# Rotary embedding for several heads at once: first and second halves of the heads in separate projection blocks, DMAs put each head together

## The chip, the cores and the metric

One core of a Trainium2 chip runs the kernel. The metric is device time in microseconds (us) of one execution. Engines are named as in the profile: PE (TensorE, the matrix engine; PEld is its weight load), DVE (VectorE), ACT (ScalarE), POOL (GpSimd) and SP (SyncE, which issues all DMAs here).

## What is computed

One inference step of a two-layer decoder trunk in float32, for a prompt of 512 tokens and 8 sample sequences of 4 tokens: 544 tokens with the same weights. Each layer normalises x, multiplies it by `w_in` (1024 to 3584 columns), rotates queries and keys, runs four retention heads of width 128 and eight attention heads of width 64, multiplies by `w_out`, and then runs a convolutional feed-forward part (`w_up`, `w_down`). The rotation is the part that is changed:

```python
def rotary(x, pos):
    half = x.shape[-1] // 2
    inv = ROPE_THETA ** (-jnp.arange(half, dtype=jnp.float32) / half)
    ang = pos.astype(jnp.float32)[:, None] * inv[None, :]
    cos = jnp.cos(ang)[None, :, None, :]
    sin = jnp.sin(ang)[None, :, None, :]
    x1, x2 = xf[..., :half], xf[..., half:]
    return jnp.concatenate([x1 * cos - x2 * sin, x2 * cos + x1 * sin], axis=-1)
def project(h, w_in_l, pos):
    z = h @ w_in_l
    qr, kr, vr, gr, qa, ka, va = jnp.split(z, SPLITS, axis=-1)
    qr, kr = rotary(hr(qr), pos), rotary(hr(kr), pos)      # 4 heads of 128
    qa, ka = rotary(ha(qa), pos), rotary(ha(ka), pos)      # 8 heads of 64
    return qr, kr, hr(vr), gr, qa, ka, ha(va)
```

## The kernel before

Activations lie transposed: 128 features are the partitions, the 544 tokens run along the free axis, in two halves of 272. A **block** is one output of 128 columns of a weight matrix. For a `w_in` block PE runs 48 matmuls of 128x272: eight pieces of the contraction, three passes (high and low parts of weight and activation: `xh` with `wh`, `xl` with `wh`, `xh` with `wl`), two token halves. The result lies in a PSUM tile `ps`. A weight block comes in two halves of 24 matmuls each: `load_w` (line 305) loads a half six halves ahead, `split_w` (311) splits it three halves ahead, the high part on ACT (`wh`), the low part on DVE (`wl`).

The blocks of a layer's mixer run in the order that `mixer` writes out (1032 to 1041): `va`, `va`, then for each pair of attention heads `ka`, `qa` (and the later `va`), then `vr`, `kr`, `qr` of each retention head, then four gates, 28 blocks in all, and after them 16 half-sized blocks of `w_out`. A block of queries or keys holds one retention head or two attention heads. When it is done, `rotary_out` (486) takes it out of PSUM: one DVE product of full height with the cosine table (`ra`); DVE products with the sine table that read one half of a head and write to the partitions of the other half (`rb`: four of 32 partitions in an attention block, two of 64 in a retention block); and POOL adds the two, a part of 512 tokens and a part of 32. The result is the finished head tile. The tables have the norm's factor folded in, by POOL (`fold_tables`, 539).

Between the steps of this main stream other pieces of work are placed: attention of a pair of heads (`att_pair`, 544, which first copies queries and keys into high and low parts, `qq` and `kk` on ACT, `qq` and `kl` on DVE, and then runs four `att_unit` pieces: products, softmax over DVE and ACT, transposes of `p`, products with `vt`), the sample attention, the retention heads (`ret_head`, 740). Their PE work goes to PSUM tiles called `sec`. Where they stand is decided while the program is built: `Stream` (152) keeps an estimated time for each engine (`Clock`, 60, with costs in `charge`, 115) and places a piece where that estimate says that its operands are there. On the chip each engine then runs its own list in order. Attention of pairs 0 and 2 is one sequence (`pairs`, 919), of pairs 1 and 3 another, and the sample attention follows both. Tiles of one size share 51 buffers (`blk`, 245).

Of the kernel before, what the change touches and what calls it, by code (L numbers as in the profile page):

```python
# [9 lines left out]
F32 = mybir.dt.float32  # L10
# [3 lines left out]
PSUM = bass.MemoryType.PSUM  # L14
# [3 lines left out]
NT = SEQ + NB * T  # L18
HC = NT // 2
PC = SEQ // 2  # L20
SC = NB * T // 2
KB = D // 128
ZB = 28
FB = 22
GROUPS = ((0, 5), (5, 10), (10, 14), (14, 18), (18, 22))
# [34 lines left out]
class Clock:  # L60
    """Estimates when each engine reaches and ends the instructions that were traced, so that
    independent work is traced where its operands are likely to be there."""

# [30 lines left out]
class Engine:  # L94
    """Hands instructions on to an engine of the core and to the clock."""

# [55 lines left out]
class Stream:  # L152
    """Places pieces of independent work between the steps of the main product stream. A generator
    yields what its next piece needs: its kind (the tensor engine, another engine, or a condition),
    its operands and its banks of PSUM."""

# [68 lines left out]
def trunk(ctx: ExitStack, tc: tile.TileContext, xin, w_in, w_out, w_up, w_down, kc, vc, s0, sctx_d, params_d,  # L225
# [19 lines left out]
    def blk(shape, dt=F32, s="b"):  # L245
        return work.tile(shape, dt, name=name(s), tag="blk", bufs=NBLK)
# [10 lines left out]
    def store(dst, src):  # L257
        def gen():
            sp.dma_start(dst, src)
            return  # L260
            yield
        st.spawn(gen(), "store", EW("sp", src))
# [28 lines left out]

# [1 line left out]
    main = []  # L293
# [41 lines left out]

# [1 line left out]
    x = [cpool.tile([128, 2, HC], F32, name=f"x{n}") for n in range(KB)]  # L337
# [13 lines left out]

# [1 line left out]
    class Norm:  # L353
# [47 lines left out]
        def rsqrt(self, ps, shape):  # L401
            """Yields its steps; returns 1 / sqrt(mean + eps), with a Newton step on the table's value."""
            r, v, t = (blk(shape, F32, s) for s in ("rstd", "var", "tmp"))
            yield EW("act", *ps)
            for c, p in enumerate(ps):
                act.activation(r[:, c], p[:, :HC], AF.Ln, bias=eps, scale=1.0 / D)
            act.activation(r, r, AF.Exp, scale=-0.5)
            for c, p in enumerate(ps):
                dve.tensor_scalar(v[:, c], p[:, :HC], -0.5 / D, -0.5 * EPS, op0=OP.mult, op1=OP.add)
            done(len(ps))  # L410
            yield EW("dve", r)
            dve.tensor_mul(t, r, r)
            yield EW("dve", t)
            dve.tensor_mul(t, t, v)
            yield EW("dve", t)
            dve.scalar_tensor_tensor(r, t, 1.5, r, op0=OP.add, op1=OP.mult)
            return r
# [10 lines left out]
    class Last(Norm):  # L428
        """Takes the last product stream by halves of the tokens."""

# [46 lines left out]

# [1 line left out]
    def two(ap, w):  # L479
        return ap.rearrange("p (c n) -> p c n", c=2)  # L480
# [4 lines left out]

    def rotary_out(ps, cos, sin, half, dst):
        a = blk([128, 2, HC], F32, "ra")
        b = blk([128, 2, HC], F32, "rb")
        dve.tensor_mul(a, ps[:, :, :HC], cos)
        for q in range(0, 128, 2 * half):  # L490
            lo, hi = slice(q, q + half), slice(q + half, q + 2 * half)
            dve.tensor_mul(b[lo], ps[hi, :, :HC], sin[hi])
            dve.tensor_mul(b[hi], ps[lo, :, :HC], sin[lo])
        pool.tensor_add(two(dst[:, 0:SEQ], PC), a[:, :, 0:PC], b[:, :, 0:PC])
        pool.tensor_add(two(dst[:, SEQ:NT], SC), a[:, :, PC:HC], b[:, :, PC:HC])

# [27 lines left out]

# [1 line left out]
    class Layer:  # L526
# [15 lines left out]

    # prompt attention of one pair of heads
    def att_pair(L, l, hp):
# [12 lines left out]
        done(2)  # L557
        # float32 products as f32r parts: [q hi; q lo] x [k hi; k hi], then q hi x k lo
        qs, ks = [], []
# [71 lines left out]

    # sample attention of four sequences; rows are (sequence, head, token)
    def att_sample(L, l, g):
# [104 lines left out]

    # retention of one head
    def ret_head(L, l, h):  # L740
# [31 lines left out]
        done()  # L772
        # sample parts of this head
        yield PE(k, v, q, banks=1)
# [122 lines left out]

# [1 line left out]
    def mixer(l):  # L899
# [63 lines left out]
        def va(hp):  # L963
            def evac(ps):
                if hp == 0:
                    fold_tables(L, 2, norm)
                L.va[hp] = blk([128, NT], F32, "va")
                scaled_out(ps, norm.rstd, L.va[hp])
                store(kv_o[l, 1, hp], L.va[hp])
            return evac  # L970

        def ka(hp):
            def evac(ps):
                L.ka[hp] = blk([128, NT], F32, "ka")
                rotary_out(ps, *L.tab[2], 32, L.ka[hp])
                pool.tensor_copy(L.ks[:, hp, :], L.ka[hp][:, SEQ:])
                store(kv_o[l, 0, hp], L.ka[hp])
            return evac

        def qa(hp):  # L980
            def evac(ps):
                L.qa[hp] = blk([128, NT], F32, "qa")
                rotary_out(ps, *L.tab[2], 32, L.qa[hp])
                for s in range(2):
                    r = slice(64 * s, 64 * s + 64)
                    c = (2 * hp + s) * T
                    pool.tensor_copy(L.qpad[r, hp, :, c:c + T],
                                     L.qa[hp][r, SEQ:].rearrange("p (b t) -> p b t", b=NB))
                L.cat[4 + hp] = blk([128, 2, HC], F32, "cat")
                L.have.add(("qa", hp))  # L990
                if hp == 2:
                    start_ret()
                if hp == 3:
                    L.tab.pop(2)
                    rope_tables(L, l, 0)()
                    fold_tables(L, 0, norm)
            return evac

# [11 lines left out]
        def vr(h):  # L1010
            def evac(ps):
                L.vr[h] = blk([128, NT], F32, "vr")
                scaled_out(ps, norm.rstd, L.vr[h])
            return evac

        def kr(h):
            def evac(ps):
                L.kr[h] = blk([128, NT], F32, "kr")
                rotary_out(ps, *L.tab[0], 64, L.kr[h])
            return evac  # L1020

        def qr(h):
            def evac(ps):
                L.qr[h] = blk([128, NT], F32, "qr")
                rotary_out(ps, *L.tab[0], 64, L.qr[h])
                L.cat[h] = blk([128, 2, HC], F32, "catr")
                L.have.add(("qr", h))
                if h == 3:
                    L.tab.pop(0)
            return evac  # L1030

        rhs = rhs_of(norm)
        order = [(24, va(0)), (25, va(1))]
        for hp in range(4):
            order += [(24 + hp, va(hp))] * (hp > 1) + [(20 + hp, ka(hp)), (16 + hp, qa(hp))]
        for h in range(4):
            order += [(8 + h, vr(h)), (4 + h, kr(h)), (h, qr(h))]
        for h in range(4):
# [39 lines left out]

# [1 line left out]
    def ffn(l):  # L1080
# [98 lines left out]

# [1 line left out]
    first = norms[0][0]  # L1181
# [3 lines left out]
    sp.dma_start(par, params_d[:, :NPAR])  # L1185
    # keeps the tensor engine's clock up until the first operands are there
    warm = sec([128, 512])
# [32 lines left out]

    # the first two blocks run side by side while x arrives
    main[0]["pre"]()
# [40 lines left out]

    # the last products run by halves of the tokens, so that the first half's norm and output overlap the second
    main[-KB]["pre"]()
# [20 lines left out]
def _tables():  # L1286
# [51 lines left out]
    for first, half in ((0, 64), (2, 32)):  # L1338
        e = (-np.arange(half, dtype=f) / f(half)).astype(f)
        inv = np.power(10000.0, e.astype(np.float64)).astype(f)  # L1340
        ang = (p[None, :] * inv[:, None]).astype(f).astype(np.float64)
        cos, sin = _chunk(np.cos(ang).astype(f)), _chunk(np.sin(ang).astype(f))
        rope[:, first] = np.concatenate([cos] * (128 // half))
        rope[:, first + 1] = np.concatenate([sin, -sin] * (64 // half))
    return out, rope
# [8 lines left out]
def _layout(i):  # L1354
    g = {k: np.asarray(v) for k, v in i.items()}
    a = {}
    tok = np.concatenate([g["x_prompt"].reshape(SEQ, D), g["x_sample"].reshape(NB * T, D)])
    a["xin"] = _chunk(tok.T.reshape(KB, 128, NT).transpose(1, 0, 2))

    def w(n):  # L1360
# [51 lines left out]
```

## Time and profile before

| what | us |
|---|---|
| median of 3 runs | 1456.33 |
| lowest and highest run | 1456.01, 1456.38 |
| profiled execution, first to last instruction (span) | 1455.7 |
| PE busy in the span | 1428.8 (98%) |
| DVE busy | 975.1 (67%) |
| ACT busy | 598.8 (41%) |
| POOL busy | 183.1 (13%) |

The three runs and the profiled execution are different executions. Of the profiled one no time but its span is given; the median of the runs is 0.6 us above that span, and this 0.6 us is taken as what lies around the span. A busy PE in the profile is not a PE at its peak: a matmul's end is modelled, and it is shown until well after the next one has begun. So gaps below some 0.2 us do not show as idle time of PE.

### The profile page before, as it was taken

How to read it: one execution, taken by the hardware profiler on the slowest of the kernel's cores; microseconds unless marked ns; L12 is line 12 of the kernel's file. 1: busy time of each engine (PE TensorE's matmuls, PEld its weight loads, DVE VectorE, ACT ScalarE, POOL GpSimd, SP SyncE). 2: the span in 40 equal slices, each digit the busy share in tenths (PEclk: the TensorE clock that was granted, in tenths of full speed). 3: DMA queues.
4: the chain of work that ended last, by engine and by line, in shares of the span. 5: the costliest groups of instructions: out<-in, count | busy, mean ns of one | idle time of the engine just before them, and what ended most of it. 6: DMA issues, size and time to landing. Idle time of an engine off the chain costs nothing.

```text
span 1455.7 us, 29739 instructions
## 1 busy us (share of the span) xinstructions
PE 1428.8 (98%) x11634; PEld 1364.1 (94%) x11634; DVE 975.1 (67%) x1889; ACT 598.8 (41%) x1156; POOL 183.1 (13%) x553
## 2 busy tenths in 40 slices
PE   8998999999999999999999999999999999999997
PEld 8987887999999999999998888889999999999996
DVE  8977645588775565656678776446977746566665
ACT  4456423444443333323434554224544424333334
POOL 4323211000000000000023221110000000000003
PEclk9999999999999999999999999999999999999999
DMA  6232387433223223223322234863332231322231
GB/s 235 97 104 87 105 275 285 153 123 109 88 81 94 87 75 103 95 83 106 107 90 91 95 103 140 319 230 115 124 111 88 70 118 63 102 87 96 86 98 62
DMA packets 98635, 173.92 MB, mean 119 GB/s; under 512 B 11072, under 2 KB 21440, under 8 KB 98496
## 3 DMA queue, kind: packets, MB, share of 16 engines
q1 hardware_dynamic: 98496, 172.03, 35.1%
q8 instruction: 92, 1.51, 0.4%
q14 instruction: 47, 0.39, 0.1%
HBM read 159.77 MB, written 12.21 MB: 118 GB/s over the span
## 4 chain that ended last, share of the span: by engine, by line
PE 89%; DVE 7%; issue 2%; ACT 1%; DMA 1%; SPq 0%; DVEq 0%; ACTq 0%
PE ps L112 78%; PE sec L112 11%; DVE rb L112 2%; DVE wl L112 2%; DVE p L112 1%; DVE qq L112 0%; DMA kt<-kc 0%; DMA x<-xin 0%; DVE ra L112 0%; ACT p L112 0%; SPq L112 0%; DVE kl L112 0%; DVE xl L112 0%; DVE pm L112 0%; DVE sq L112 0%
## 5 line engine op out<-in xcount | busy, mean ns | idle before, releaser
L112 PE MATMUL ps<-xh,wh 128*128 128x272 f32 x2304 | 490.7, 294 | 1.3 <-ACT wh L112 1.1
L112 PE MATMUL ps<-xh,wl 128*128 128x272 f32 x2304 | 478.1, 289 | 1.4 <-DVE wl L112 1.4
L112 PE MATMUL ps<-xl,wh 128*128 128x272 f32 x2304 | 476.8, 288 | 0.0
L112 PEld LDWEIGHTS ps<-xh,wh 128*128 128x128 f32 x2304 | 362.4, 190 | 12.4 <-issue 7.8
L112 PEld LDWEIGHTS ps<-xh,wl 128*128 128x128 f32 x2304 | 362.4, 189 | 1.6 <-DVE wl L112 1.6
L112 PEld LDWEIGHTS ps<-xl,wh 128*128 128x128 f32 x2304 | 362.4, 189 | 0.1
L112 ACT ACTIVATE wh<-raw 128x512 fp32r<-128x512 f32 (+2 forms) x432 | 247.7, 598 | 172.1 <-PE ps L112 155.9
L112 DVE TENSOR_TENSOR wl<-raw,wh 128x512 fp32r<-128x512 f32 (+2 forms) x432 | 296.7, 705 | 18.4 <-ACT wh L112 17.6
L112 DVE SCALAR_TENSOR_TENSOR c<-u,taps,c 128x560 f32<-128x560 f32 x176 | 141.1, 802 | 88.6 <-ACT c L112 85.5
L112 ACT ACTIVATE c<-u,taps 128x560 f32<-128x560 f32 x88 | 75.4, 856 | 226.6 <-DVE u L112 223.2
L112 DVE TENSOR_TENSOR x<-x,ps 128x544 f32<-128x544 f32 (+1 forms) x120 | 81.6, 680 | 119.8 <-PE ps L112 119.3
L112 PE MATMUL ps<-yh,wh 128*128 128x272 f32 x704 | 150.9, 288 | 0.0
L112 PE MATMUL ps<-yh,wl 128*128 128x272 f32 x704 | 150.5, 288 | 0.0
L112 PE MATMUL ps<-yl,wh 128*128 128x272 f32 x704 | 150.4, 288 | 0.0
L112 DVE TENSOR_TENSOR u<-ps,rstd 128x512 f32<-128x512 f32 (+1 forms) x176 | 69.1, 435 | 80.3 <-PE ps L112 80.3
L112 PEld LDWEIGHTS ps<-yl,wh 128*128 128x128 f32 x704 | 112.2, 188 | 0.1
L112 PEld LDWEIGHTS ps<-yh,wh 128*128 128x128 f32 x704 | 112.2, 188 | 0.1
L112 PEld LDWEIGHTS ps<-yh,wl 128*128 128x128 f32 x704 | 112.2, 188 | 0.0
L112 POOL COPY last<-u 128x2 f32<-128x2 f32 (+1 forms) x176 | 28.0, 191 | 665.6 <-DVE u L112 658.8
L112 DVE TENSOR_TENSOR rb<-ps,rope 32x544 f32<-32x544 f32 (+1 forms) x96 | 69.2, 721 | 1.4
L112 ACT ACTIVATE yh<-y 128x544 fp32r<-128x544 f32 x44 | 29.0, 658 | 82.6 <-DVE y L112 82.6
L112 ACT ACTIVATE p<-p,pm 128x128 f32<-128x128 f32 (+3 forms) x64 | 35.5, 556 | 58.6 <-DVE pm L112 57.1
(153 smaller groups left out, 1439.4 us busy)
## 6 DMA issues: line engine op xcount, KB each, us to landing
raw<-w_up SPq DMA_DIRECT2D x176, 256.0 KB, 2.8
raw<-w_in SPq DMA_DIRECT2D x112, 256.0 KB, 3.6
kt<-kc SPq DMA_DIRECT2D x80, 256.0 KB, 4.6
vt<-vc SPq DMA_DIRECT2D x80, 256.0 KB, 4.8
raw<-w_down SPq DMA_DIRECT2D x48, 256.0 KB, 2.7
raw<-w_out SPq DMA_DIRECT2D x32, 256.0 KB, 2.9
raw<-w_down SPq DMA_DIRECT2D x32, 192.0 KB, 2.4
s<-s SPq DMA_DIRECT2D x16, 256.0 KB, 5.5
```

Of the source, the lines that this page charges most:

```text
L112: return f(*args, **kw)
```

## The change

The columns of `w_in` for queries and keys are put in another order on the host, so that one block holds the first halves of two retention heads (or of four attention heads) and the next block their second halves. The blocks now run by groups: two `va`, two `ka`, two `qa`, two `va`, two `ka`, two `qa`, then two `vr`, two `kr`, two `qr`, twice. `rotated` replaces `rotary_out`. After the first block of a couple DVE multiplies it by cosine and sine (two products of full height, kept in `ra`), after the second likewise (`rb`); POOL forms the difference and the sum (`r1`, `r2`), with the same two parts each. DMAs on SP then copy 32 (or 64) partitions each out of `r1` and `r2` into the head tiles: eight for a couple of attention blocks, four for a couple of retention blocks. The code that used the finished tile right away (`after`) is now recorded after those DMAs.

```diff
-    def rotary_out(ps, cos, sin, half, dst):
-        a = blk([128, 2, HC], F32, "ra")
-        b = blk([128, 2, HC], F32, "rb")
-        dve.tensor_mul(a, ps[:, :, :HC], cos)
-        for q in range(0, 128, 2 * half):
-            lo, hi = slice(q, q + half), slice(q + half, q + 2 * half)
-            dve.tensor_mul(b[lo], ps[hi, :, :HC], sin[hi])
-            dve.tensor_mul(b[hi], ps[lo, :, :HC], sin[lo])
-        pool.tensor_add(two(dst[:, 0:SEQ], PC), a[:, :, 0:PC], b[:, :, 0:PC])
-        pool.tensor_add(two(dst[:, SEQ:NT], SC), a[:, :, PC:HC], b[:, :, PC:HC])
+    def rotated(tabs, half, dsts, after):
+        kept = []
+
+        def first(ps):
+            kept.extend(blk([128, 2, HC], F32, "ra") for _ in range(2))
+            for t, tab in zip(kept, tabs()):
+                dve.tensor_mul(t, ps[:, :, :HC], tab)
+
+        def second(ps):
+            bs = [blk([128, 2, HC], F32, "rb") for _ in range(2)]
+            for t, tab in zip(bs, tabs()):
+                dve.tensor_mul(t, ps[:, :, :HC], tab)
+            outs = [blk([128, NT], F32, n) for n in ("r1", "r2")]
+            for o, x0, x1, f in ((outs[0], kept[0], bs[1], pool.tensor_sub), (outs[1], bs[0], kept[1], pool.tensor_add)):
+                f(two(o[:, 0:SEQ], PC), x0[:, :, 0:PC], x1[:, :, 0:PC])
+                f(two(o[:, SEQ:NT], SC), x0[:, :, PC:HC], x1[:, :, PC:HC])
+            kept.clear()
+            tiles = dsts()
+
+            def gather(outs):
+                yield EW("sp", *outs)
+                per = 128 // (2 * half)
+                for i, d in enumerate(tiles):
+                    for j in range(per):
+                        for n, o in enumerate(outs):
+                            q = 2 * half * j + half * n
+                            p = half * (i * per + j)
+                            sp.dma_start(d[q:q + half], o[p:p + half])
+                after(tiles)
+            st.spawn(gather(outs), "evac")
+
+        return first, second
...
-        order = [(24, va(0)), (25, va(1))]
-        for hp in range(4):
-            order += [(24 + hp, va(hp))] * (hp > 1) + [(20 + hp, ka(hp)), (16 + hp, qa(hp))]
-        for h in range(4):
-            order += [(8 + h, vr(h)), (4 + h, kr(h)), (h, qr(h))]
+        order = []
+        for i in range(2):
+            order += [(24 + 2 * i, va(2 * i)), (25 + 2 * i, va(2 * i + 1))]
+            order += [*zip((20 + 2 * i, 21 + 2 * i), ka(i)), *zip((16 + 2 * i, 17 + 2 * i), qa(i))]
+        for i in range(2):
+            order += [(8 + 2 * i, vr(2 * i)), (9 + 2 * i, vr(2 * i + 1))]
+            order += [*zip((4 + 2 * i, 5 + 2 * i), kr(i)), *zip((2 * i, 2 * i + 1), qr(i))]
...
-        rope[:, first + 1] = np.concatenate([sin, -sin] * (64 // half))
+        rope[:, first + 1] = np.concatenate([sin] * (128 // half))
```

Three places show how the recorded order moves. In the names a number tells buffers apart; `ps` is a block's result, `sec` a product of a side piece, `cst` the constants.

**DVE, first layer, where the last attention block before the retention blocks is rotated.** `ps_1256` is that block's result, `ps_1287` the one with the change; `wl` are low parts of weight halves, `p` and `pm` belong to the softmax. Before:

```order
L112 TENSOR_TENSOR ra_1350<-ps_1256,rope_189 128x544
L112 TENSOR_TENSOR rb_1351<-ps_1256,rope_191 32x544 x4
L112 TENSOR_TENSOR wl_1372<-raw_1160,wh_1371 128x512
L112 TENSOR_TENSOR wl_1408<-raw_1257,wh_1407 128x512
L112 ISA p_1423,pm_1424<-sec_1381,cst_81 128x128
L112 ISA pm_1424 128x1
L112 ISA p_1432,pm_1433<-sec_1383,cst_81 128x128
L112 ISA pm_1433 128x1
L112 ISA p_1437,pm_1438<-sec_1328,cst_81 128x384
```

With the change:

```order
L113 RECIPROCAL pm_1324<-pm_1324 128x1
L113 TENSOR_SCALAR p_1323<-p_1323,pm_1324 128x512
L113 TENSOR_TENSOR wl_1347<-raw_1145,wh_1346 128x512
L113 TENSOR_TENSOR rb_1398<-ps_1287,rope_189 128x544
L113 TENSOR_TENSOR rb_1399<-ps_1287,rope_191 128x544
L113 TENSOR_TENSOR wl_1420<-raw_1222,wh_1419 128x512
L113 TENSOR_TENSOR wl_1450<-raw_1288,wh_1449 128x512
L113 TENSOR_TENSOR vr_1517<-ps_1416,rstd_312 128x512
```

Five products of a block have become two. Before, softmax pieces of three units stood right behind them; with the change the softmax of pairs 0 and 1 stands ahead of them and none follows at once.

**SP, first layer, after the second block of `qa` (with the change).** `qa_108` and `qa_109` are the first two query tiles, `raw` weight halves; the list at the end of a row names what it waits for.

```order
L113 DMA raw_119_671<-w_in 128x512 [waits DVE_49]
L113 DMA qa_108_632<-r1_106_626 32x544 [waits Pool_49]
L113 DMA qa_108_632<-r2_107_627 32x544 [waits Pool_49]
L113 DMA qa_108_632<-r1_106_626 32x544 [waits DMAHW0_49]
L113 DMA qa_108_632<-r2_107_627 32x544 [waits DMAHW1_49]
L113 DMA qa_109_633<-r1_106_626 32x544 [waits DMAHW2_49]
L113 DMA qa_109_633<-r2_107_627 32x544 [waits DMAHW3_49]
L113 DMA qa_109_633<-r1_106_626 32x544 [waits DMAHW4_49]
L113 DMA qa_109_633<-r2_107_627 32x544 [waits DMAHW5_49]
L113 DMA raw_138_745<-w_in 128x512 [waits DMAHW6_49,DVE_49]
```

Before there were only the loads and the stores of the caches here; a weight load now stands in line behind eight transfers, which wait for POOL.

**PE, the first attention products of the first pair.** Before they stood a quarter into block 6, and the block that ends the query tile was block 3. With the change the query tile ends with block 5, and `kk` stands 21 rows into block 7 (`ps_744`):

```order
L113 MATMUL ps_744<-xl_171,wh_643 128x272 x2
L113 MATMUL ps_744<-xh_169,wl_644 128x272 x2
L113 MATMUL sec_815<-kk_714,qq_715 128x128
L113 MATMUL sec_817<-kk_775,qq_776 128x128
L113 MATMUL sec_815<-kl_713,qq_715 128x128
L113 MATMUL sec_817<-kl_713,qq_776 128x128
L113 MATMUL ps_744<-xh_173,wh_643 128x272 x2
```

So between the end of the query tile's last block (5) and this place lie block 6 with ten transposes of `va` beside it, and 42 of the 48 matmuls of block 7. The same distance stands ahead of pairs 2 and 3 (from block 11 into block 13), and in the second layer. Pairs 0 and 1 run side by side from here on, the second one unit behind, in blocks 7 to 11, and pairs 2 and 3 in blocks 13 to 17; before, the four pairs were spread over blocks 6 to 18. The retention heads begin in block 18, before in block 14; in both orders all of this work ends in blocks 25 to 27, ahead of `w_out`.

## Rows read from the trace of the kernel before

**Rows 1.** The page: busy time per engine, and the largest group of products.

```profile
PE 1428.8 (98%) x11634; PEld 1364.1 (94%) x11634; DVE 975.1 (67%) x1889; ACT 598.8 (41%) x1156; POOL 183.1 (13%) x553
...
L112 PE MATMUL ps<-xh,wh 128*128 128x272 f32 x2304 | 490.7, 294 | 1.3 <-ACT wh L112 1.1
```

**Rows 2.** Busy time by stretches: length, engines (instructions), granted clock, DMA share, GB/s.

```profile
24.57:50.16 25.59, 25.34 (x204) 25.12 (x203) 25.20 (x32) 9.42 (x17) 10.87 (x11) 1.00 0.33 114
...
740.44:890.81 150.37, 144.50 (x1129) 131.35 (x1127) 118.47 (x261) 72.86 (x185) 35.85 (x46) 0.98 0.31 101
400.00:450.00 50.00, 50.00 (x400) 50.00 (x399) 34.61 (x62) 20.63 (x33) 4.01 (x32) 1.00 0.23 75
```

**Rows 3.** Instructions grouped by line and form, DVE: the rotary products, both layers.

```profile
L112 DVE TENSOR_TENSOR rb<-ps,rope 32x544 f32<-32x544 f32 x64 | 46.1, 720 | 0.9
...
L112 DVE TENSOR_TENSOR rb<-ps,rope 64x544 f32<-64x544 f32 x32 | 23.1, 722 | 0.5
L112 DVE TENSOR_TENSOR ra<-ps,rope 128x544 f32<-128x544 f32 x32 | 23.1, 721 | 37.8 <-PE ps L112 37.6
```

**Rows 4.** Waits of PE: in total, times, longest.

```profile
PE sec L112 <- DVE p L112: 9.3, 12, 2.2
PE sec L112 <- DVE qq L112: 2.2, 3, 0.8
```

**Rows 5.** Timeline of DVE, POOL and PE around 109 us: start, length, what.

```profile
105.51 0.72 DVE L112 TENSOR_TENSOR ra<-ps,rope 128x544 f32<-128x544 f32 x1
106.25 2.92 DVE L112 TENSOR_TENSOR rb<-ps,rope 32x544 f32<-32x544 f32 x4
109.20 2.39 DVE L112 TENSOR_TENSOR wl<-raw,wh 128x512 fp32r<-128x512 f32 x2
...
109.31 2.38 POOL L112 TENSOR_TENSOR qa<-ra,rb 128x512 f32<-128x512 f32 x2 [6.29 <-DVE rb L112]
...
113.77 0.33 PE L112 MATMUL sec<-cst,p 128*128 128x128 f32 x1 [2.17 <-DVE p L112]
```

**Rows 6.** Grouped by line and form, DVE: all low parts of that size.

```profile
L112 DVE TENSOR_TENSOR wl<-raw,wh 128x512 fp32r<-128x512 f32 x368 | 268.0, 743 | 18.4 <-ACT wh L112 17.6
```

**Rows 7.** Timeline of PE: three more waits of the first layer.

```profile
60.73 0.30 PE L112 MATMUL sec<-cst,p 128*128 128x128 f32 x1 [1.03 <-DVE p L112]
...
143.15 0.66 PE L112 MATMUL sec<-cst,p 128*128 128x128 f32 x4 [0.48 <-DVE p L112]
...
145.57 0.30 PE L112 MATMUL sec<-kk,qq 128*128 128x128 f32 x1 [0.81 <-DVE qq L112]
```

**Rows 8.** Busy time by stretches, second layer: two falls of the clock.

```profile
829.46:832.87 3.41, 3.41 (x18) 2.81 (x17) 2.93 (x8) 0.81 (x5) 0.57 (x1) 0.50 0.00 0
...
863.60:867.00 3.40, 3.40 (x17) 3.40 (x16) 2.30 (x8) 2.48 (x11) 0.00 (x0) 0.50 0.12 43
```

**Rows 9.** Grouped by line and form: POOL's sums, the splits of queries and keys.

```profile
L112 POOL TENSOR_TENSOR qa<-ra,rb 128x512 f32<-128x512 f32 x8 | 14.0, 1748 | 41.9 <-DVE rb L112 31.2 <-issue 5.4 <-ACT wh L112 5.3
L112 POOL TENSOR_TENSOR qr<-ra,rb 128x512 f32<-128x512 f32 x8 | 11.1, 1388 | 58.2 <-ACT kd L112 18.8 <-DVE rb L112 14.6 <-PE ps L112 12.5
L112 POOL TENSOR_TENSOR qa<-ra,rb 128x32 f32<-128x32 f32 x8 | 5.6, 701 | 0.0
...
L112 ACT ACTIVATE qq<-qa 64x512 fp32r<-64x512 f32 x16 | 10.0, 625 | 7.8 <-POOL qa L112 7.6
...
L112 DVE TENSOR_TENSOR kl<-ka,kk 64x512 fp32r<-64x512 f32 x16 | 11.1, 691 | 0.5
```

**Rows 10.** DMAs: the stores of one 64 KB tile, and SP's timeline from 30 us.

```profile
L112 SPq DMA_DIRECT2D pret_o<-ss x8: 343/343/344, 153.0 to 966.5; - x8
...
DMA to landing us min/median/max: 1.5/1.5/3.1
...
30.20 1.04 SPq L112 DMA_DIRECT2D kv_o<-va  x2
```

**Rows 11.** Timeline of PE's weight load: five transposes of `va`.

```profile
36.99 0.54 PEld L112 LDWEIGHTS sec<-cst,va 128*128 128x128 f32 x5
```

More of the change, by code (lines that the diff above doesn't have):

```diff
@@ L23 @@
 ZB = 28
+D_IN = ZB * 128
 FB = 22
@@ L970, in va, with ka, tiles, after @@
             return evac
[L972 to L991, printed above, removed]
+        def ka(g):
+            def tiles():
+                return [blk([128, NT], F32, "ka") for _ in range(2)]
+            def after(t):
+                for hp, k in zip((2 * g, 2 * g + 1), t):
+                    L.ka[hp] = k
+                    pool.tensor_copy(L.ks[:, hp, :], k[:, SEQ:])
+                    store(kv_o[l, 0, hp], k)
+            return rotated(lambda: L.tab[2], 32, tiles, after)
+        def qa(g):
+            def tiles():
+                return [blk([128, NT], F32, "qa") for _ in range(2)]
+            def after(t):
+                for hp, q in zip((2 * g, 2 * g + 1), t):
+                    L.qa[hp] = q
+                    for s in range(2):
+                        r = slice(64 * s, 64 * s + 64)
+                        c = (2 * hp + s) * T
+                        pool.tensor_copy(L.qpad[r, hp, :, c:c + T], q[r, SEQ:].rearrange("p (b t) -> p b t", b=NB))
+                    L.cat[4 + hp] = blk([128, 2, HC], F32, "cat")
+                    L.have.add(("qa", hp))
+            first, second = rotated(lambda: L.tab[2], 32, tiles, after)
+            def last(ps):
+                second(ps)
+                if g == 0:
                     start_ret()
-                if hp == 3:
+                else:
                     L.tab.pop(2)
@@ L996, in evac @@
                     fold_tables(L, 0, norm)
-            return evac
+            return first, last
         def g(h):
@@ L1014, in vr, with kr, tiles, after @@
             return evac
[L1016 to L1028, printed above, removed]
+        def kr(g):
+            def tiles():
+                return [blk([128, NT], F32, "kr") for _ in range(2)]
+            def after(t):
+                L.kr[2 * g:2 * g + 2] = t
+            return rotated(lambda: L.tab[0], 64, tiles, after)
+        def qr(g):
+            def tiles():
+                return [blk([128, NT], F32, "qr") for _ in range(2)]
+            def after(t):
+                for h, q in zip((2 * g, 2 * g + 1), t):
+                    L.qr[h] = q
+                    L.cat[h] = blk([128, 2, HC], F32, "catr")
+                    L.have.add(("qr", h))
+            first, second = rotated(lambda: L.tab[0], 64, tiles, after)
+            def last(ps):
+                second(ps)
+                if g == 1:
                     L.tab.pop(0)
-            return evac
+            return first, last
         rhs = rhs_of(norm)
-        order = [(24, va(0)), (25, va(1))]
-        for hp in range(4):
-            order += [(24 + hp, va(hp))] * (hp > 1) + [(20 + hp, ka(hp)), (16 + hp, qa(hp))]
-        for h in range(4):
-            order += [(8 + h, vr(h)), (4 + h, kr(h)), (h, qr(h))]
+        order = []
[5 more added lines that the diff above has]
+            order += [*zip((4 + 2 * i, 5 + 2 * i), kr(i)), *zip((2 * i, 2 * i + 1), qr(i))]
         for h in range(4):
@@ L1358, in _layout @@
     a["xin"] = _chunk(tok.T.reshape(KB, 128, NT).transpose(1, 0, 2))
+    z = np.arange(D_IN)
+    for at, heads, half in ((0, 2, 64), (512, 2, 64), (2048, 4, 32), (2560, 4, 32)):
+        z[at:at + 512] = z[at:at + 512].reshape(2, heads, 2, half).transpose(0, 2, 1, 3).reshape(-1)
+    g["w_in"] = g["w_in"][:, :, z]
     def w(n):
```

## Prediction, made before the changed kernel had run

> **What bounds the kernel now.** I read the engine shares first [rows 1]: PE is busy 98% of the span, no other engine over 67%. So time can only be won where PE waits or runs below its pace, and lost where something makes it wait. The pace comes from the stretches [rows 2]: in the feed-forward part PE starts 400 matmuls of a block in 50.00 us, 0.125 us each, 6.0 us for a block of 48. The second layer's mixer, blocks 2 to 17, has 144.50 us of PE in 150.37 us: 5.9 us idle, and the clock's mean is 0.98, not 1.00. A busy DVE alone costs nothing: from 24.57 to 50.16 us it worked 25.20 of 25.59 us, yet PE went on with 204 matmuls, its full pace, because nothing there waited for DVE at once [rows 2].
>
> The waits say for what PE stood: 9.3 us in 12 waits for softmax rows `p`, 2.2 us in 3 for `qq` [rows 4], 11.5 us together. The timeline shows how the largest arises [rows 5]: at 105.51 DVE begins a query block's products, one of 0.72 us and four that take 2.92; then come two low parts, 2.39 us; only then the softmax for which PE has stood 2.17 us at 113.77. Two things hold DVE there. The rotation is one: 3.64 us. The other is POOL: its sums of the same block run from 109.31 for 2.38 us, and the two low parts take 2.39 us where two of the mean length take 1.49 [rows 5, 6]. So 0.9 us of DVE's time beside a pair of sums is lost.
>
> Three more waits of the first layer are of this kind [rows 7]: 1.03 us at 60.73 (behind the products of block 5), 0.48 and 0.81 us at 143.15 and 145.57 (beside the sums and the first scaling of a retention query tile). The second layer has the same four, each within 0.02 us. There the clock also stands at 0.50, its lower level of 1.2 GHz, in two pieces of 3.4 us, one from 829.46, just behind the twin of the 2.17 us wait, one from 863.60, behind the twins of the last two [rows 8]; 18 and 17 matmuls start there where 27 would.
>
> **DVE: 64 products for 128.** A product takes 0.72 us with 32, 64 or 128 partitions [rows 3]. Before: 23.1 + 46.1 + 23.1 = 92.3 us. After: two of full height per block, 32 blocks, 64 x 0.72 = 46.1 us. DVE has 46.2 us less to do, 23.1 in each layer. Almost none of it is on the path by itself; what it can buy are the waits. In an attention block five products become two: 3.64 us become 1.44, and the softmax stands 2.2 us earlier, as much as the longest wait. The retention heads now begin after the softmax of the last pair, so the waits of 0.48 and 0.81 us lose their cause.
>
> **What I take as gain.** The four waits: 2.17 + 1.03 + 0.48 + 0.81 = 4.5 us, in two layers 9.0. A wait ends with one matmul shown at 0.294 us that goes on at 0.125 [rows 1, 2], so 0.17 for each of eight waits, 1.4. Two pieces at half clock cost half of 3.4 us each, 3.4. Sum 13.8 us. Bounds: only the two waits of 2.2 us, 4.4; or all 11.5, with 15 times 0.17 (2.5) and the clock, 17.4. I don't take all, since the softmax chain of DVE, ACT and DVE remains, and the attention of two pairs now stands in ten blocks of a layer instead of thirteen.
>
> **The new chain: query tile to its first product.** From the end of block 5: 0.3 us until the last matmul is out, two products 1.44, then POOL. It has as many sums as before, but now two pairs in a row, 2 x (1.75 + 0.70) = 4.90 [rows 9]: done at 6.64 us. SP then issues; the nearest rows are stores, 0.34 us each for a 64 KB tile and 0.52 for a whole head tile (two in 1.04) [rows 10], and I take the longer. The first head tile needs four transfers, one of which can go before the second sum; the fourth is issued at 6.64 + 2 x 0.52 = 7.68. The nearest tile lands 1.5 us after issue, at most 3.1 [rows 10]: 9.2 with 1.5, the median. ACT makes six copies, 6 x 0.625 = 3.75, and DVE the last difference, 0.69 [rows 9]: 13.6 us. By the new order PE gets there after block 6 (6.0), ten transposes at 0.11 [rows 11] and 42 matmuls at 0.125: 12.35 us. So PE waits 1.25 us, twice in each layer: **5.0 us**. It is 0 where sums and issues go at their shorter lengths (1.39 and 0.34), 2.85 each (11.4) with 3.1 us of landing.
>
> The third retention head reads its query tile directly. Its chain ends at 6.64 + 1.5 = 8.1 us; PE gets there after 36 matmuls (4.5) and eight transposes (0.9), 5.4 us, and eight small products. The first head has a whole block more. Wait between 0 and 2.7 us, 4.3 with the long landing; I take 1.5, in two layers **3.0 us**.
>
> **The sums beside the softmax.** Before, ten rotated blocks of a layer set off their sums while a pair's softmax ran, and four waits came of it. Now two couples do (they end with blocks 9 and 15), four blocks' worth: 4/10 of four waits, about 0.6 us each, in two layers some **2.0 us**; 0 if no `p` falls beside them, 7.2 if each of eight long sums holds DVE 0.9 us on the path.
>
> **Edits at nothing, with their cover.** On SP the 96 transfers (32 and 16 in a layer) wait for POOL, and the stores of `ka` for the landing; behind them stand weight loads, which are six halves, 18 us, ahead, against some 12 us for the whole chain. If that cover went, the split and then PE would wait. On ACT `qq` waits for the landing with a split of `wh` behind it; splits are three halves, 9 us, ahead, and the wait is a few us. On POOL the copies of the key and query samples wait for the landing; the next sums come two blocks (12 us) later. The later begin of the attention (block 7, not 6) costs nothing while all of it ends before `w_out`, which it does in both orders. Tables, buffers and the columns' order on the host add no instruction to the path.
>
> **Sum.** -13.8 + 5.0 + 3.0 + 2.0 = -3.8 us. The profiled execution spans 1455.7 us and 0.6 lies around it (the median of the runs, 1456.33, is that sum): 1455.7 - 3.8 + 0.6 = **1452.5 us**. A measurement here can tell 0.2%, 2.9 us, from no change, so this is faster by little more than that.
>
> For the landing the Trainium skill has another figure: "DMA: Bandwidth & Descriptors", section "Anatomy of one DMA — SWDGE (gpsimd) path", gives about 2.0 us plus the bytes over 436 GB/s, for transfers that GpSimd issues. An estimate by that page is 2.16 us for 32x544; no row here moves a tile within the core, so the trace can't show which holds. By it each of the six waits would be 0.66 us longer, and the sum 4.0 us higher, about 1456.5.
>
> **Rivals.** *The gather decides (slower).* The chain through POOL, SP and the transfers is longer than I take it; the transfers share the engines with weight loads, and the only spread shown reaches 3.1 us [rows 10]. Then the waits are 4 x 2.85 + 2 x 4.3 = 20.0 us, and with two new falls of the clock (3.4) and the 2.0: 25.4 - 13.8 = +11.6, 1467.9 us. It decides from the point where the six waits average (13.8 - 2.0) / 6 = 2.0 us; I have 1.3. For it: every link is added in series, none of it is in a row of before as a whole. Against: a median landing of 1.5 us. Chance 0.27.
>
> The clock makes it dearer: it fell behind a wait of 2.19 us in the second layer, and did not behind the 2.17 us in the first. The Trainium skill, "TensorE: Matmul & The Clock Gate", section "HAM oscillation — how this bites in real kernels", says that waits for DMAs between products bring the clock down and the next work starts cold; the trace agrees in one layer of two, and by the rule the rival's price could grow by 1.7 us for each of its other four waits.
>
> *DVE was not the cause (no change).* The chain of softmax steps, now of two pairs side by side in fewer blocks, makes PE wait where DVE's products did. Only the two waits of 2.2 us and one fall of the clock (1.7) go, 6.1, against 8.0 of gathers: +1.9, 1458.2 us. For it: the waits name `p`, whose chain also runs over ACT. Chance 0.12.
>
> *The gathers stay hidden (faster).* Sums and issues go at their short lengths and all named waits go: 1455.7 + 0.6 - 17.4 = 1438.9 us. For it: 46.2 us less on DVE, and side pieces are placed by estimates that leave some room. Chance 0.16.
>
> *The change doesn't do what it says:* a product of full height would cost more than one of 32 partitions. The rows of 32, 64 and 128 partitions exclude it [rows 3]; chance 0.02, then no change.
>
> **From cases to numbers.** The forecast has 0.43; its own range, 1446 to 1459, comes from one landing more or less and the bounds of the gain, and I put 0.25 of it below 1453.4 (faster), 0.14 within 0.2%, 0.04 above. With the rivals: faster 0.25 + 0.16 + 0.02 of the second = 0.43; same 0.14 + 0.06 + 0.02 = 0.22; slower 0.04 + 0.04 + 0.27 = 0.35. The range, 1440 to 1466, leaves out the far end of the first rival and of the third, about 0.1 each.
>
> **What would show it.** In the profile after: `ra` and `rb` as 64 products of 128x544 at 0.72 us, DVE at 929 us; waits of PE for `p` well under 9.3 us in total, none of 2 us behind a rotary block; new waits of `sec` at the first `kk` of pairs 0 and 2, about 1.25 us, which lead over ACT's `qq` to a DMA; transfers of 32x544 with some 0.5 us of issue and 1.5 of landing; the clock at 1.00 where it stood at 0.50. I am wrong where the landing is far from 1.5 us, where waits for `p` stay at 9 us, or where PE waits for `wh`, `wl` or `raw`, whose cover I counted as enough.

## The result, and the profile after

| | before | with the change |
|---|---|---|
| median, us | 1456.36 (1456.01 to 1456.99) | 1447.39 (1445.69 to 1448.63) |
| span of the profiled execution | 1455.7 | 1445.6 |

The ratio is 0.9937, interval 0.9923 to 0.9951: 9.0 us faster, where 3.8 were forecast: the time lies inside the stated range of 1440 to 1466, and the change is 2.4 times the forecast one. Each run of the changed kernel carries its span, which is 2.1 us below its time; so the 0.6 us that the prediction put around the span was too little, and the profiled execution of before was some 1.4 us slower than its median. Of the 10.1 us between the two spans about 1 is that.

The page's busy times after the change:

```profile
PE 1426.0 (99%) x11634; PEld 1363.0 (94%) x11634; DVE 913.3 (63%) x1825; ACT 598.1 (41%) x1156; POOL 175.5 (12%) x553
```

PE's waits after the change (in total, times, longest):

```profile
PE sec L113 <- DMA qr<-r: 2.8, 2, 1.7
PE sec L113 <- DVE p L113: 2.8, 4, 0.7
```

The waits for `p` have fallen from 9.3 to 2.8 us and those for `qq` from 2.2 to nothing [rows 4]. Waits for the retention query tile are new. DVE lost 61.8 us of work, not 46.2. Its products, grouped by line and form, and the low parts of [rows 6]:

```profile
L113 DVE TENSOR_TENSOR wl<-raw,wh 128x512 fp32r<-128x512 f32 x368 | 258.2, 716 | 34.4 <-ACT wh L113 34.3
...
L113 DVE TENSOR_TENSOR rb<-ps,rope 128x544 f32<-128x544 f32 x32 | 21.7, 719 | 44.4 <-PE ps L113 38.8 <-issue 5.7
L113 DVE TENSOR_TENSOR ra<-ps,rope 128x544 f32<-128x544 f32 x32 | 21.7, 718 | 25.9 <-PE ps L113 25.9
```

The rotation fell from 92.3 to 43.4 us. The same 368 low parts take 9.8 us less, since fewer of them run beside POOL's sums and products (some 30 in place of some 50; why that matters, see below).

Both mixers from block 2 to `w_out`, as stretches; before:

```profile
24.57:276.19 251.62, 244.60 (x2066) 214.31 (x2065) 175.45 (x403) 108.37 (x263) 57.31 (x89) 1.00 0.47 162
740.44:993.11 252.67, 246.80 (x2067) 216.72 (x2065) 170.15 (x396) 107.36 (x261) 53.98 (x87) 0.99 0.47 160
```

With the change (the third row is a piece of the second, behind the wait that ends at 947.43):

```profile
23.89:271.13 247.24, 243.97 (x2066) 214.10 (x2065) 144.60 (x371) 108.02 (x263) 54.03 (x89) 1.00 0.55 181
734.66:981.64 246.98, 243.87 (x2066) 215.15 (x2065) 139.18 (x364) 106.89 (x261) 49.78 (x87) 0.99 0.55 181
...
949.15:952.50 3.35, 3.35 (x17) 3.35 (x17) 0.94 (x4) 1.88 (x6) 1.24 (x9) 0.51 0.00 0
```

PE runs the same matmuls in stretches 4.4 and 5.7 us shorter, 10.1 in all: 6.5 of it is PE's idle time (12.9 before, 6.4 after), most of the rest is one fall of the clock less (one now, two in [rows 8]) and fewer slow first matmuls, since fewer waits are left. So the whole gain lies in the two mixers. The question for the runs is what removed the waits.

The chain that the prediction had costed, from the end of block 5 (48.51 us) to the first product of a pair, as timeline of several engines:

```profile
48.71 1.36 DVE L113 TENSOR_TENSOR rb<-ps,rope 128x544 f32<-128x544 f32 x2 [3.48 <-PE ps L113]
...
50.15 2.33 POOL L113 TENSOR_TENSOR r<-ra,rb 128x512 f32<-128x512 f32 x2 [2.15 <-DVE rb L113]
52.45 1.48 POOL L113 TENSOR_TENSOR r<-rb,ra 128x512 f32<-128x512 f32 x2
...
52.51 5.77 SPq L113 DMA_DIRECT2D qa<-r  x8
...
56.15 0.63 ACT L113 ACTIVATE qq<-qa 64x512 fp32r<-64x512 f32 x1 [0.57 <-DMA qa<-r]
58.52 1.26 ACT L113 ACTIVATE kk<-ka 64x512 fp32r<-64x512 f32 x2
...
59.41 0.69 DVE L113 TENSOR_TENSOR kl<-ka,kk 64x512 fp32r<-64x512 f32 x1
...
60.92 0.34 PE L113 MATMUL sec<-kk,qq 128*128 128x128 f32 x2
```

DVE's last difference ends at 60.10, 11.6 us after the block; the prediction had 13.6. PE comes at 60.92, 12.4 us after, as forecast, and doesn't wait: 0.8 us to spare.

### The profile page after: what moved, and what is told of

Read it like the earlier page. It is cut to its first block, busy times and chain, and to the rows that moved or that the text cites. A ratio compares the mean times of both kernels' runs of the same rounds, so it can differ in the third digit from the quotient of the medians.

```text
span 1445.6 us, 29883 instructions
## 1 busy us (share of the span) xinstructions
PE 1426.0 (99%) x11634; PEld 1363.0 (94%) x11634; DVE 913.3 (63%) x1825; ACT 598.1 (41%) x1156; POOL 175.5 (12%) x553
## 4 chain that ended last, share of the span: by engine, by line
PE 93%; DVE 3%; DMA 2%; issue 1%; SPq 0%; POOL 0%; DVEq 0%; ACT 0%; POOLq 0%; ACTq 0%
PE ps L113 83%; PE sec L113 11%; DVE p L113 1%; DMA qr<-r 1%; DMA x<-xin 0%; DVE rb L113 0%; DMA vt<-vc 0%; SPq L113 0%; DVE wl L113 0%; POOL r L113 0%; DVE sq L113 0%; DVE xl L113 0%; DVE va L113 0%; DVEq L1449 0%; DVE tmp L113 0%
## 5 line engine op out<-in xcount | busy, mean ns | idle before, releaser
L113 DVE TENSOR_TENSOR wl<-raw,wh 128x512 fp32r<-128x512 f32 (+2 forms) x432 | 286.9, 682 | 34.4 <-ACT wh L113 34.3
L113 POOL TENSOR_TENSOR r<-ra,rb 128x512 f32<-128x512 f32 (+1 forms) x32 | 33.5, 1067 | 254.9 <-DVE rb L113 120.3
L113 PE MATMUL ps<-ch,wh 128*128 128x272 f32 x256 | 53.4, 290 | 0.0
```

The lines of the kernel that those rows point to most:

```text
L113: return f(*args, **kw)
```

## The experiments

All times are medians; "mixers" is the length of both stretches in the profiled execution (before 504.3, changed 494.2 us).

| kernel | us | ratio to before, interval | mixers |
|---|---|---|---|
| new order, old rotation | 1443.24 | 0.9896 to 0.9925 | 488.8 |
| attention's order alone | 1446.40 | 0.9917 to 0.9947 | 492.9 |
| retention's order alone | 1459.00 | 1.0008 to 1.0028 | 505.7 |
| products twice, placing unaware | 1466.76 | 1.0054 to 1.0096 | 511.0 |
| products twice, placing aware | 1441.25 | 0.9881 to 0.9910 | 488.2 |
| before, 1.2 us of room | 1442.88 | 0.9893 to 0.9926 | 489.4 |
| changed, 1.2 us of room | 1441.50 | 0.9885 to 0.9914 | 486.5 |
| changed, retention later | 1443.39 | 0.9899 to 0.9929 | 488.1 |
| four transfers more | 1459.85 | 1.0015 to 1.0034 | 504.3 |
| sums on DVE | 1440.46 | 0.9874 to 0.9907 | 489.5 |
| sums on DVE, room | 1448.26 | 0.9932 to 0.9961 | 492.8 |
| the same, retention later | 1445.24 | 0.9904 to 0.9932 | 494.1 |

### Order without the new rotation

```diff
-                if hp == 2:
+                if hp == 1:
                     start_ret()
...
-        order = [(24, va(0)), (25, va(1))]
-        for hp in range(4):
-            order += [(24 + hp, va(hp))] * (hp > 1) + [(20 + hp, ka(hp)), (16 + hp, qa(hp))]
-        for h in range(4):
-            order += [(8 + h, vr(h)), (4 + h, kr(h)), (h, qr(h))]
+        order = []
+        for i in (0, 2):
+            order += [(24 + i, va(i)), (25 + i, va(i + 1)), (20 + i, ka(i)), (21 + i, ka(i + 1))]
+            order += [(16 + i, qa(i)), (17 + i, qa(i + 1))]
+        for i in (0, 2):
+            order += [(8 + i, vr(i)), (9 + i, vr(i + 1)), (4 + i, kr(i)), (5 + i, kr(i + 1))]
+            order += [(i, qr(i)), (i + 1, qr(i + 1))]
```

(`start_ret` only sets up small tiles of the retention heads; it now comes after the second pair, as in the changed kernel.)

> The old rotation (five or three products of DVE for a block, sums at once, no transfers) in the new order of blocks. If the gain came from halving DVE's products, the waits for the softmax rows stay: over 6 us for p in total, and the time is 1452 to 1458 us. If the order alone brought it (softmax away from the rotation, retention heads after it), waits for p fall to about 3 us and the time is 1445 to 1449 us.

1443.24 us, with DVE at 974.2 us of work, as before. PE's waits in this kernel:

```profile
PE sec L112 <- DVE qq L112: 0.7, 2, 0.5
PE sec L112 <- DVE p L112: 0.7, 2, 0.3
```

The theory that only halving DVE's products removes the waits fell here: the order alone gives 13.1 us, more than the whole change. In the new order the new rotation with its transfers costs 4.2 us (1443.2 to 1447.4).

> The kernel before with the attention blocks alone in the new order (two va, two ka, two qa, twice); retention blocks in their old order, old rotation. Of the waits before, 2.17 and 1.03 us of each layer belong to attention blocks and 0.48 and 0.81 to the first retention block. If each part of the order removes its own waits, this one takes 2 x 3.2 us, their tails (0.7) and one fall of the clock (1.7): 1456.4 - 8.8, about 1447.6 us. If the gain of the order is the later begin of the retention heads, little goes: 1453 to 1457 us.

> The kernel before with the retention blocks alone in the new order (two vr, two kr, two qr, twice); attention blocks in their old order, old rotation. If each part removes its own waits: 2 x 1.3 us, their tails (0.7) and the second fall of the clock (1.7): about 1451.4 us. If the whole gain is in the retention heads' later begin: 1443 to 1446 us.

The two halves of that edit. Attention's order alone took 1446.4, near the 1447.6 of its own waits. Retention's order alone, expected at 1451.4, made the kernel slower, with more waits for `p` than before:

```profile
PE sec L112 <- DVE p L112: 12.6, 15, 2.2
```

So a part of an order need not remove "its" waits; each order places all pieces anew.

### DVE's work

```diff
             for t, tab in zip(kept, tabs()):
                 dve.tensor_mul(t, ps[:, :, :HC], tab)
+                nc.vector.tensor_mul(t, ps[:, :, :HC], tab)
```

(and the same behind the second block; `nc.vector` goes past the estimate, `dve` would go through it)

> The changed kernel with each of the 64 rotary products run twice, so that DVE has its old 92 us of rotation back; order of blocks and transfers are the changed kernel's. If DVE's time mattered, each couple's chain is 1.4 us longer and the softmax behind it as much later: the four waits of 0.7 us for p become about 2 us each (+5.6), the two waits for the third retention head grow by 1.4 each (+2.9), and the attention's first products, which have 0.8 us to spare, wait 0.6 each (+2.6): about 1457 us. If DVE's work was hidden anyway: 1447 to 1449 us.

1466.76 us: 19 us slower than the changed kernel, twice the 9.6 us expected. Waits of PE in this kernel:

```profile
PE sec L113 <- DVE p L113: 9.2, 12, 1.1
PE sec L113 <- DMA qr<-r: 2.6, 2, 1.8
PE sec L113 <- ACT kk L113: 1.8, 3, 1.0
```

In its first mixer the clock also falls twice. Taken alone this run says that DVE's work decides, and for a fixed list of PE it does. The next has the same work, known to the estimate (`dve` in place of `nc.vector`):

> The changed kernel with each rotary product run twice, as in the run before of this kind, but now the estimate that places the pieces knows of the second one. If 46 us more of DVE cost time by themselves, it stays near that run's 1466.8 us, at least above 1455. If only work that the placing does not know of costs time, it comes back to the changed kernel, 1446 to 1450 us, and halving the products is then worth nothing in itself.

The rotary products of this kernel, by line and form:

```profile
L113 DVE TENSOR_TENSOR rb<-ps,rope 128x544 f32<-128x544 f32 x64 | 44.8, 721 | 18.0 <-PE ps L113 16.9
L113 DVE TENSOR_TENSOR ra<-ps,rope 128x544 f32<-128x544 f32 x64 | 44.8, 721 | 14.2 <-PE ps L113 13.1
```

and its waits of PE for `p`:

```profile
PE sec L113 <- DVE p L113: 0.5, 3, 0.2
```

1441.25 us: with twice the products it is 6 us faster than the changed kernel. The waits of the changed kernel are all but gone, those for `qr` too, since all pieces are laid anew. So the 46 us of DVE that the change saves bring no gain that this pair of runs shows; what costs time is a piece on PE that stands earlier than its operands come.

### Room in the placing

A piece of attention may stand on PE where the estimate has its operands 1.2 us earlier, in place of 0.3 (`MARGIN`). It is a single line, in the old kernel and in the changed one:

```diff
-            return max(self.clock.when(kind, aps), self.bank_free(banks)) + MARGIN <= now
+            return max(self.clock.when(kind, aps), self.bank_free(banks)) + (1.2 if g[1][:3] == "att" else MARGIN) <= now
```

> The kernel before, order and rotation untouched, but attention pieces are placed where the estimate has their operands 1.2 us earlier than PE (0.3 before). If the waits come from pieces that stand too early, because the estimate lacks what POOL's sums do to DVE, the waits for p fall from 9.3 us to under 4 and the time to 1443 to 1448 us, without the new order of blocks. If the order of blocks itself is needed, waits stay over 7 us and the time at 1452 to 1457 us.

> The changed kernel with the same 1.2 us for attention pieces. The four waits of 0.7 us for p go (2.8 and some tails); the wait for the third retention head's tile (2.8) and its fall of the clock (1.7) stay, unless the heads move later with the attention, then they go too: 1444 us with them, 1440 without. If the later attention pushes the rest past block 27, 1447 us or more.

The old kernel, with its order, its five products for a block and no transfer, took 1442.88 us with this line; its waits for `p` fell from 9.3 to:

```profile
PE sec L112 <- DVE p L112: 2.8, 4, 1.3
```

The changed kernel took 1441.5, with no wait for `p` of note left in its profile and none for `qr`, since the heads moved later too. So the waits of before were pieces placed too early. The estimate charges 1.23 us for a long sum of POOL, which took 1.75 [rows 9], and nothing for what the sum does to DVE; 0.9 us more of room is about enough to cover that. With the same room in both, the whole change is worth 1.4 us (1442.9 to 1441.5). So most of its 9.0 us came from laying all pieces anew, not from the rotation; the order alone says the same.

### What the changed kernel lost again

```diff
                             sp.dma_start(d[q:q + half], o[p:p + half])
+                    if half == 64:
+                        clock.wrote[clock.key(d)] = ("sp", clock.wrote[clock.key(d)][1] + 4.0)
```

> The changed kernel, but the estimate that places the pieces takes the retention tiles to land 4 us later, so that products with them stand later on PE. No work is changed. If the wait of PE for the third head's query tile is what is left to win, its 2.8 us and the fall of the clock behind it (1.7) go: 1442 to 1445 us. If the retention heads then end too late for the output blocks, new waits take their place in blocks 26 to 28 and the time stays at 1446 to 1450 us.

1443.39 us: 4.0 less than the changed kernel, and the waits for `qr` and the fall of the clock in the mixer are gone, as the first theory had it. Where the wait came from, in the changed kernel's timelines:

```profile
219.88 5.92 SPq L113 DMA_DIRECT2D vt<-vc  x8
...
229.43 1.91 SPq L113 DMA_DIRECT2D qr<-r  x2
...
238.43 0.79 PE L113 MATMUL sec<-qr,kr 128*128 128x128 f32 x5 [1.07 <-DMA qr<-r]
...
947.43 0.79 PE L113 MATMUL sec<-qr,kr 128*128 128x128 f32 x5 [1.74 <-DMA qr<-r]
```

and by tile, attention's query transfers first, retention's below:

```profile
L113 SPq DMA_DIRECT2D qa<-r x32: 513/588/1919, 52.5 to 824.0; - x32
...
DMA to landing us min/median/max: 1.9/2.0/3.8
...
L113 SPq DMA_DIRECT2D qr<-r x16: 461/467/587, 165.6 to 942.0; - x16
...
DMA to landing us min/median/max: 5.7/6.4/8.3
```

The retention transfers stand behind loads of the sample caches, 3 to 7 of which are still on their way when one is issued, and they take three times as long. They are also twice as large, but the size isn't the reason. In the kernel with products twice, placing aware, at most one such load is on its way, and the same tiles land as follows:

```profile
L113 SPq DMA_DIRECT2D qr<-r x16: 467/494/1797, 160.6 to 938.9; - x16
...
DMA to landing us min/median/max: 2.2/2.4/3.8
```

To test how much room the attention's transfers have, four tiny ones are put ahead of them:

```diff
+                for j in range(4 * (half == 32)):
+                    nc.sync.dma_start(spare[32 * j:32 * j + 32], outs[1][32 * j:32 * j + 32, :8])
```

> The changed kernel with four tiny transfers (32 partitions of 8 values, into a tile that nothing reads) on SP ahead of each attention couple's eight, unknown to the estimate that places the pieces. By the trace of the changed kernel DVE ends its last difference 0.8 us before PE's first product of a pair. Four issues of about 0.55 us then make PE wait 2.2 - 0.8 = 1.4 us at four places: 1447.4 + 5.6 = 1453 us. If the transfers were hidden with more to spare than that: 1446 to 1449 us.

Timeline of SP and PE in this kernel, first pair:

```profile
54.24 2.42 SPq L514 DMA_DIRECT2D spare<-r  x4
56.72 5.32 SPq L113 DMA_DIRECT2D qa<-r  x8
...
63.13 0.33 PE L113 MATMUL sec<-kk,qq 128*128 128x128 f32 x1 [1.50 <-ACT kk L113]
```

At the four places PE waits 1.5 us, close to the 1.4 expected; one of them has 0.8 more (7.0 us for `kk` in all). The time rose by 12.5, not 5.6: the profiled execution's span rose by 9.8, of which these waits are 7.0, the slow matmuls behind them some 1.0 and longer waits for `p` 0.9; the rest stays open. The clock falls once in the mixers of either kernel, here in the first one. The four read `r2`, so no transfer of a head can start ahead of the second sum any more, which the expectation had not counted. The attention's transfers are hidden, but with little left.

### POOL's sums

```diff
-            for o, x0, x1, f in ((outs[0], kept[0], bs[1], pool.tensor_sub), (outs[1], bs[0], kept[1], pool.tensor_add)):
+            for o, x0, x1, f in ((outs[0], kept[0], bs[1], dve.tensor_sub), (outs[1], bs[0], kept[1], dve.tensor_add)):
```

> The changed kernel with the sums on DVE instead of POOL: 2 x (0.69 + 0.18) = 1.7 us of DVE for a couple, where POOL takes 3.7 and holds DVE's scalings and low parts beside it. If POOL's sums are what holds DVE, the scalings of p at blocks 10 and 16 fall from 1.3 and 1.5 us to 0.4, the transfers start 2 us earlier, and the two waits for the third retention head (2.8) shrink: 1442 to 1446 us. If DVE's own time counts more than POOL's hold on it, the waits for p stay or grow, 1447 to 1450 us.

In the changed kernel the four waits of 0.7 us look like this (timeline of DVE, POOL and PE, block 10, first layer):

```profile
86.01 1.33 DVE L113 TENSOR_SCALAR p<-p,pm 128x512 f32<-128x512 f32 x1
87.45 1.52 DVE L113 TENSOR_SCALAR p<-p,pm 128x512 f32<-128x512 f32 x1
...
85.47 1.98 POOL L113 TENSOR_TENSOR r<-ra,rb 128x512 f32<-128x512 f32 x2 [25.30 <-PE sec L113]
87.41 1.67 POOL L113 TENSOR_TENSOR r<-rb,ra 128x512 f32<-128x512 f32 x2
...
89.12 0.63 PE L113 MATMUL sec<-cst,p 128*128 128x128 f32 x4 [0.70 <-DVE p L113]
...
99.05 0.49 DVE L113 TENSOR_SCALAR p<-p,pm 128x512 f32<-128x512 f32 x1
```

Beside the sums a scaling takes 1.3 to 1.5 us, away from them 0.49. The timeline of DVE with the sums there, same block:

```profile
85.03 0.79 DVE L113 TENSOR_TENSOR r<-ra,rb 128x512 f32<-128x512 f32 x2
85.74 0.79 DVE L113 TENSOR_TENSOR r<-rb,ra 128x512 f32<-128x512 f32 x2
...
87.24 0.49 DVE L113 TENSOR_SCALAR p<-p,pm 128x512 f32<-128x512 f32 x1
```

DVE does 1.6 us more for a couple and gets it back at once. 1440.46 us, a little better than expected: 7 us below the changed kernel, and the lowest time here, though products twice, placing aware (1441.25) and the changed kernel with room (1441.5) are too close to be told from it. The edit goes through the estimate, so all pieces are laid anew here too, and no run separates that from what the sums did to DVE: the scalings beside the sums are faster, but how much of the 7 us that is stays open. Its waits for `p` are still 2.2 us, at new places beside POOL's folding of the tables.

> The changed kernel with the sums on DVE and the same 1.2 us for attention pieces. The kernel with the sums on DVE alone took 1440.5 us and has waits of 2.2 us for p left: they go, 1438 to 1440 us. If what is left is not in these waits, 1440 to 1442 us.

> The run before with the sums on DVE and 1.2 us for attention pieces took 1448.3 us: its waits for p are gone, but PE waits 5.5 us in two places where a retention head's products stand ahead of the landing of its query tile, and the clock falls for 6.8 us behind one of them (3.4 lost). This kernel takes the retention tiles to land 4 us later in the estimate as well, nothing else. If that wait is all that is wrong with it: 1448.3 - 5.5 - 3.4 = 1439.4 us, as fast as the fastest here (1440.5) or a little faster. If the heads then end too late for the output blocks: 1442 us or more.

Adding room to this kernel lost time twice. 1448.26: no wait for `p`, but waits in two places before a retention head's product, and a fall of the clock around the longer one:

```profile
PE sec L113 <- ACT rv L113: 5.5, 2, 3.0
```

With the later landing in the estimate 1445.24, scattered from 1441.8 to 1448.0; the waits for `rv` are nearly gone and two for `p`, 2.3 and 2.4 us, are new. In the first, ACT stood 5 us before `rv`, the copy of a value tile, until the transfers of `qr` had landed (its timeline):

```profile
163.37 0.60 ACT L113 ACTIVATE rv<-sec 128x512 f32<-128x512 f32 x1 [4.97 <-DMA qr<-r]
```

`rv` doesn't read `qr`. Its list of waits names two DMA queues, so its buffer, one of the 51, was probably a source of the transfers. That is read from the program and not shown: no run with another buffer was made.

## Why the prediction was right, and where it was not

- **What bounds the kernel** held: the gain lies in PE's waits and the clock, and nowhere else.
- **"What I take as gain", 13.8 us,** was too small for this pair of profiles: no wait of before for `p` or `qq` is left, which the prediction had as its upper bound, 17.4. In their place came seven other waits: 2.8 us for `qr`, 2.8 for `p` and 0.6 for a tile of the sample caches, with 0.17 behind each and one fall of the clock (1.7), 9.1 in all. The difference is 8.3, against 9.0 measured.
- **Its cause was wrong.** The step "what it can buy are the waits: in an attention block five products become two" failed: most of the waits also go with five products (new order, or 1.2 us of room in the old one), and doubled products cost nothing once the placing knows them. The view of the 2.17 us wait [rows 5] showed what DVE did before the late softmax. It didn't show that PE's piece stood too early; that it could stand later at no cost, a run had to show. The 1.03 us wait, put down to products, had POOL's sums at work too: two low parts ahead of it took 2.40 us instead of 1.49.
- **"So PE waits 1.25 us, twice in each layer: 5.0 us"** is the term that failed: it measured 0. The forecast of -3.8 without this 5.0 would have been -8.8, near the measured -9.0, but by luck: the gain was 3.6 larger than taken, and the other waits cost 9.1 where 3.0 and 2.0 were taken. In the chain of 13.6 us POOL's sums took 3.8 instead of 4.9, since DVE stood idle during the second pair, and ACT's six copies with DVE's difference 3.95 instead of 4.44, since they overlap. The landing was 0.5 longer (2.0, not 1.5), and the first transfers left before the second sum was done.
- For the landing the prediction gave an estimate of 2.16 us by the Trainium skill, "DMA: Bandwidth & Descriptors", section "Anatomy of one DMA — SWDGE (gpsimd) path". The trace agrees for attention (2.0 us) and not for retention (6.4), where cache loads stood ahead; with at most one of those on its way the retention tiles took 2.4 (products twice, placing aware).
- **"The third retention head … 3.0 us"** measured 2.8, but by luck, as two errors cancel: the landing was 6.4 us, not 1.5, and PE came 9.6 us after its block in the first layer and 8.0 in the second, not 5.4. The fall of the clock behind it (1.7) was left out.
- **"The sums beside the softmax … 2.0 us"**: 2.8 us, four waits of 0.7 at the two couples named, blocks 9 and 15.
- **Edits at nothing**: SP's weight loads, ACT's splits and POOL's copies made no new wait of PE in the mixers. The loads of the sample caches, which also stand behind the transfers on SP, were not considered; one new wait of 0.6 us is for such a tile.
- **The rivals**: "the gather decides" was wrong for the kernel as it stands, but 0.8 us from true: four tiny transfers more turned 9 us of gain into a loss. "The gathers stay hidden" came nearest for attention, and all named waits did go; it left out the waits that came instead. "DVE was not the cause" named half of the truth; its price was wrong, because it let the waits stay.

## What to carry to other kernels

Where pieces are placed by an estimate, a wait on the bottleneck engine may say only that the piece stands too early; try the placing with a little more room before making its operands cheaper. More room is no rule: it won 13.5 us in the old kernel and 5.9 in the changed one, and lost 7.8 with the sums on DVE. A change that reorders such a program moves every piece, so a few us can come from the new places alone; test the order without the rest, and add work with the estimate told of it and not told. Before splitting work onto another engine, see what that engine's operation does to its neighbour.

## What the runs showed of the hardware that was not expected

- POOL's sums hold some operations of DVE and not others: a scaling of 128x512 took 0.49 us alone and 1.3 to 1.5 beside them, and two low parts 2.39 instead of 1.49 [rows 5, 6], while an operation that reads PSUM kept its length: 0.73 us for the two rotary products that ran beside a sum (products twice, placing unaware), 0.72 otherwise. The Trainium skill, "SBUF — State Buffer", section "SBUF: two separate sides", has this as an exclusive lock of a port pair for a whole instruction; the rows agree.
- A transfer of 68 KB within the core took 0.59 us of SP to issue and 2.0 us to land; one of 136 KB took 2.4 us to land with at most one cache load on its way, and 6.4 us with 3 to 7.
- The clock fell behind a wait of PE of 1.74 us in the changed kernel and not behind one of 1.07; before, it fell behind 2.19 and not behind 2.17. The length of a single wait doesn't decide it: the second fall of before [rows 8] came behind waits of 0.50 and 0.81 us, and with the sums on DVE and room the clock stayed at 1.00 behind one of 2.51 (timeline of PE, then the stretch):

```profile
164.02 0.71 PE L113 MATMUL sec<-qr,kr 128*128 128x128 f32 x4 [2.51 <-ACT rv L113]
...
164.02:170.00 5.98, 5.98 (x49) 5.72 (x50) 4.77 (x15) 4.05 (x13) 1.61 (x8) 1.00 0.02 4
```
